# A two-layer decoder trunk: feed-forward operands without the norm's row, quarters formed in PSUM, and two plain gate/up pairs a layer

## Chip, cores and metric

The kernel runs on one core of one Trainium2 chip. The metric is device time in microseconds. The kernel before takes 1182.96 us, the median of 3 runs (1182.89 to 1183.12).

## What is computed

Inputs and output are float32; there are 512 tokens of 1024 channels. Layer 0 mixes tokens by dilated attention, layer 1 by a causal pooling mixer; each is followed by a SwiGLU feed-forward with 2816 hidden channels. Cut to what the change touches:

```python
def rmsnorm(x, g):
    xf = x.astype(jnp.float32)
    y = xf * lax.rsqrt(jnp.mean(xf * xf, axis=-1, keepdims=True) + RMS_EPS)
    return (y * g.astype(jnp.float32)).astype(x.dtype)

def swiglu_ffn(h, w_gate_up, w_down):
    gu = h @ w_gate_up
    gate, up = gu[..., :D_FF], gu[..., D_FF:]
    return (jax.nn.silu(gate) * up) @ w_down

def reference(x, ...):
    for i in range(DEPTH):                       # DEPTH is 2
        ...
            x = x + dilated_attention_mixer(rmsnorm(x, attn_norm[j]), w_qkv[j], w_attn_out[j])
        ...
            x = x + pooling_mixer(rmsnorm(x, pool_norm[j]), w_pool_in[j], w_pool_group[j], pool_scale[j])
        x = x + swiglu_ffn(rmsnorm(x, ffn_norm[i]), w_ffn_gate_up[i], w_ffn_down[i])
    return rmsnorm(x, final_norm)
```

The norm's factor, one over the root of the mean square, is one number per token. With tokens along the free dimension it is a row, and the code calls it `row`.

## The kernel before

**Layout.** Activations stand transposed: `X[k]` holds 128 channels (partitions) by 512 tokens (columns), for k = 0 to 7. Every float32 operand of TensorE (PE) is split into a high and a low part, `split` (L92): ScalarE (ACT) rounds the value to the matmul's type, VectorE (DVE) subtracts. A product then takes three matmuls: high by high, high by low, low by high (L328 to L331, L461 to L463).

**Plain products.** `Product` (L300) multiplies a 128-channel block of weights with all 512 columns of an operand, over k; each matmul has 512 columns. A plain gate/up pair is one such product for 128 gate channels and one for 128 up channels, 8 values of k each.

**Strassen pairs.** `chained` (L521) does a pair of output blocks by Strassen's scheme in Winograd's form: outputs, weights and operands are cut into quarters, and seven multiplications named "11", "1", "2", "21", "3", "22", "4" take the place of eight. Each is `mult` (L457): 4 values of k (K2), three matmuls each, of 256 columns. Three half-banks of PSUM are used, alpha, beta and gamma; ACT copies partial sums out, DVE adds and subtracts them into SBUF tiles (L549, L554, L558). The left operands of the multiplications come from the weights (`Pair`, L157: the corners are loaded, sums of them are formed, each is split). The right ones, in the dictionary `T`, come from quarters of two channel blocks, k and k + 4.

**Preparing the operands.** `prepare` (L1122) makes `T` for one k from normalised activations: `normed` (L576) multiplies `X` by the gain and by `row`, and forms sums and differences; then four splits. As it needs `row`, it comes after the norm. `note` (L396) has by then made the operands of the plain products, gain times `X` without `row`; the plain products multiply by `row` afterwards (L1110, L1116).

**The norm.** `finish` (L436) ends the two or three leading products, and between them computes the row: squares are summed over channels by small matmuls (`rstd`, L403), DVE scales and adds eps (L414), GpSimd takes the power (L417), PE spreads the result (`spread`, L420), ACT copies it (`row_of`, L428).

**A feed-forward layer.** `ffn` (L1100) has 22 gate/up pairs j. The first NPLAIN = 4 are plain, and `prepare(j)` runs beside them; the others are Strassen pairs. The down projection goes in PARTS (L43): channels 0 to 1 plain, 2 to 9 and 10 to 17 as blocks of four `chained` calls each, 18 to 21 plain. Each block is preceded by one more gate/up pair than it needs. `operands`, `operands_right` and `operands_left` (L1149 to L1176) make the right operands of a down block; they wait in a queue `late` and run behind multiplications 4, 5 and 6 of the next `chained` call.

**Order of work.** The program's order is written by hand; engines run in the order that the scheduler fixes when the program is built. Weights flow through rings of buffers (`BUFS`): five of `w`, two of `half`, four of `raw`, two of `rawhalf`. `pump` (L207) issues loads as buffers come free and takes one step of splitting; it is called behind every multiplication. Pairs load over SyncE's queue and accumulate one corner over GpSimd's queue (L173 to L177). Plain weights of the feed-forward are "lean": ACT makes both parts, and a GpSimd DMA accumulates (L149 to L152).

**Where things lie.** Operands get a place from `slot` (L339). With `apart` they begin APART = 28 values (112 bytes) behind the start of a slot, which Strassen operands of the feed-forward use. The weights of a pair begin `shift` values behind the start of their buffer: 0 for the feed-forward (L265, L270), 16 for attention's pairs (L222, except L252), and 16 for the weights of the last five down products (L278).

## Time and profile before

| | |
|---|---|
| median of 3 runs | 1182.96 us |
| the profiled execution's own time | 1183.39 us |
| its span, first to last instruction | 1181.4 us |
| granted clock of TensorE (mean) | 0.999 |
| busy PE, DVE, ACT, GpSimd (POOL) | 1172.5, 993.2, 752.1, 174.9 us |
| moved by DMA | 209.95 MB |

On the page, a group of instructions is a line of code with its engine, what it writes and reads, its shape and its count; then the busy time, the mean duration of one in ns, and the idle time of the engine just before it with what ended it. Matmuls overlap, each record being longer than the distance to the next, so a matmul's price is taken from a stretch of time divided by the number that start in it. In a row of a stretch stand, for each engine, busy us and, in brackets, the number of instructions; then the granted clock of TensorE (1.00 is full), the share of the DMA engines and GB/s.

In layer 0 the long run of Strassen pairs fills about 521 to 769 us of the span, in layer 1 about 902 to 1150.

### The profile page before, as it was taken

The numbers are of one execution on the slowest core, as the hardware profiler recorded it, in microseconds if no ns is written. First come the engines' busy times: TensorE is split into PE (matmuls) and PEld (weight loads), VectorE is DVE, ScalarE is ACT, GpSimd is POOL, SyncE is SP. The second block draws the span as 40 slices with busy tenths as digits, with TensorE's granted clock in tenths as the row PEclk, the third lists the DMA queues.
The fourth block names the chain that finished last, engine by engine and source line by source line (L and its number), as shares of the span: only waits on it lengthen the run. The fifth ranks groups of instructions, "written<-read, shape, count | busy, mean of one in ns | idle before, by whom it ended". The sixth has DMA issues, their size and how long they took to land.

```text
span 1181.4 us, 25585 instructions
## 1 busy us (share of the span) xinstructions
PE 1172.5 (99%) x10182; PEld 1122.5 (95%) x10182; DVE 993.2 (84%) x1747; ACT 752.1 (64%) x1341; POOL 174.9 (15%) x169
## 2 busy tenths in 40 slices
PE   9999999999999999999999999999999999999997
PEld 7899999999999989889999999988889999999997
DVE  8997978989798988799988988657789998898875
ACT  7765665656556666757756766776575776676553
POOL 2111111111111002311111111112130111111100
PEclk9999999999999999999999999999999999999999
DMA  8667656665776557957777777798595777777732
GB/s 291 161 152 198 159 152 146 175 166 143 187 176 148 144 164 204 239 107 200 192 193 194 192 206 189 201 262 207 116 204 116 187 198 196 195 191 194 197 91 72
DMA packets 85017, 209.95 MB, mean 178 GB/s; under 512 B 7953, under 2 KB 13217, under 8 KB 84897
## 3 DMA queue, kind: packets, MB, share of 16 engines
q1 hardware_dynamic: 53104, 145.63, 37.2%
q0 software_dynamic: 31504, 62.41, 32.6%
q8 instruction: 79, 1.29, 0.4%
q14 instruction: 42, 0.34, 0.1%
q10 hardware_dynamic: 288, 0.29, 0.1%
HBM read 206.19 MB, written 2.10 MB: 176 GB/s over the span
## 4 chain that ended last, share of the span: by engine, by line
PE 98%; issue 1%; DVE 0%; POOL 0%; DVEq 0%; POOLq 0%
PE ps L461 21%; PE ps L462 21%; PE ps L463 21%; PE ps L328 7%; PE ps L331 7%; PE ps L329 7%; PE ps L854 2%; PE ps L637 2%; PE ps L638 2%; PE ps L639 2%; PE ps L945 2%; PE ps L732 1%; PE ps L751 1%; PE ps L916 0%; PE ps L836 0%
## 5 line engine op out<-in xcount | busy, mean ns | idle before, releaser
L96 DVE TENSOR_TENSOR w<-raw,w 128x1024 fp32r<-128x1024 f32 x271 | 330.1, 1221 | 46.1 <-ACT w L93 42.1
L93 ACT ACTIVATE w<-raw 128x1024 fp32r<-128x1024 f32 x271 | 285.9, 1062 | 120.6 <-PE ps L463 56.7
L461 PE MATMUL ps<-far,w 128*128 128x256 f32 x896 | 246.5, 275 | 0.0
L462 PE MATMUL ps<-far,w 128*128 128x256 f32 x896 | 246.5, 275 | 0.0
L463 PE MATMUL ps<-far,w 128*128 128x256 f32 x896 | 246.4, 275 | 0.0
L461 PE MATMUL ps<-near,w 128*128 128x256 f32 x749 | 209.5, 280 | 0.0
L462 PE MATMUL ps<-near,w 128*128 128x256 f32 x749 | 207.2, 277 | 0.0
L463 PE MATMUL ps<-near,w 128*128 128x256 f32 x749 | 207.2, 277 | 0.0
L461 PEld LDWEIGHTS ps<-far,w 128*128 128x128 f32 x896 | 168.2, 188 | 0.1
L462 PEld LDWEIGHTS ps<-far,w 128*128 128x128 f32 x896 | 168.2, 188 | 0.1
L463 PEld LDWEIGHTS ps<-far,w 128*128 128x128 f32 x896 | 168.2, 188 | 0.0
L462 PEld LDWEIGHTS ps<-near,w 128*128 128x128 f32 x749 | 141.1, 188 | 0.0
L461 PEld LDWEIGHTS ps<-near,w 128*128 128x128 f32 x749 | 140.7, 188 | 0.1
L463 PEld LDWEIGHTS ps<-near,w 128*128 128x128 f32 x749 | 140.7, 188 | 0.0
L328 PE MATMUL ps<-near,w 128*128 128x512 f32 (+1 forms) x332 | 125.9, 380 | 0.0
L331 PE MATMUL ps<-near,w 128*128 128x512 f32 (+1 forms) x332 | 125.0, 376 | 0.0
L329 PE MATMUL ps<-near,w 128*128 128x512 f32 (+1 forms) x332 | 124.9, 376 | 0.0
L176 POOL DMA_DIRECT2D raw<-w_pair x36 | 43.6, 1210 | 293.4 <-DMA raw<-w_pair 130.9
L329 PEld LDWEIGHTS ps<-near,w 128*128 128x128 f32 x332 | 62.5, 188 | 11.4 <-DVE near L96 0.2
L331 PEld LDWEIGHTS ps<-near,w 128*128 128x128 f32 x332 | 62.3, 188 | 11.5
L328 PEld LDWEIGHTS ps<-near,w 128*128 128x128 f32 x332 | 62.3, 188 | 11.5 <-ACT near L93 0.4
L192 DVE TENSOR_TENSOR raw<-raw 128x512 f32<-128x512 f32 x87 | 59.4, 683 | 5.2 <-issue 5.2
(342 smaller groups left out, 2726.0 us busy)
## 6 DMA issues: line engine op xcount, KB each, us to landing
raw<-w_pair SPq DMA_DIRECT2D x80, 512.0 KB, 5.0
raw<-w_qkp SPq DMA_DIRECT2D x42, 512.0 KB, 4.5
raw<-w_pair POOLq DMA_DIRECT2D x36, 512.0 KB, 7.6
raw<-w_dblock SPq DMA_DIRECT2D x32, 512.0 KB, 4.4
raw<-w_qkp POOLq DMA_DIRECT2D x21, 512.0 KB, 7.7
rawhalf<-w_pair SPq DMA_DIRECT2D x36, 256.0 KB, 5.2
raw<-w_v SPq DMA_DIRECT2D x16, 512.0 KB, 4.1
raw<-w_dblock POOLq DMA_DIRECT2D x16, 512.0 KB, 7.7
```

The lines of the kernel that those rows point to most:

```text
L93: made = nc.scalar.activation(hi, v, AF.Copy)
L96: nc.vector.tensor_tensor(lo, v, hi.bitcast(F32), op=OP.subtract)
L176: nc.gpsimd.dma_start(self.b.rearrange("p (a c) -> p a c", a=2), self.src[:, None, 3 * n:].to_broadcast([P, 2, n]), accum_op=OP.add)
L192: nc.vector.tensor_add(a[:, :n], a[:, :n], b[:, :n])
L328: nc.tensor.matmul(self.p[:, cols], w[0][:, s], mh[:, cols], start=self.done == 0, stop=False)
L329: nc.tensor.matmul(self.p[:, cols], w[0][:, s], ml[:, cols], start=False, stop=False)
L331: nc.tensor.matmul(self.p[:, cols], w[1][:, s], mh[:, cols], start=False, stop=self.done == self.n)
L461: nc.tensor.matmul(dst, w.t[0][:, c], th, start=k == 0 and not on, stop=False, skip_group_check=on)
L462: nc.tensor.matmul(dst, w.t[0][:, c], tl, start=False, stop=False, skip_group_check=on)
L463: nc.tensor.matmul(dst, w.t[1][:, c], th, start=False, stop=k == n - 1, skip_group_check=on)
L637: nc.tensor.matmul(o, mh, wh, start=k == 0, stop=False)
L638: nc.tensor.matmul(o, mh, wl, start=False, stop=False)
```

## The change

**No row in the operands.** `prepare` now takes an operator number and works from `X` and the gains alone. "11", "21" and "22" are quarters of the operands that `note` made; only the four sums are formed and split. It can therefore run ahead of the norm: three of four `prepare` calls stand before `finish` and one behind it. In layer 1 they stand between the steps of the pooling mixer, and the channel blocks are paired in another order (`ORDER`), with the weights reordered to match when the inputs are laid out.

**The row comes in at the gate.** The gate is multiplied by `row` before Silu; up is not. The hidden values are then too large by one over `row`, so the residual stream is brought to the same scale: `grow` multiplies every `X[m]` by the reciprocal of `row`, half of them behind each of the pairs j = 2 and 3. The next norm removes the scale, with an eps of its own for each token (`floor`, passed as `least`). Before the pooling mixer `X` is multiplied by the old row.

**Quarters form in PSUM.** In `chained`, ACT copies alpha into beta, and DVE writes b - d into gamma; multiplications "21" and "22" accumulate on them. What the caller does with the finished halves is passed in as `ready`: multiplying by the row and Silu for a gate, adding to `X` for a down block. Beta is one bank for the whole layer, `kept`, which held a leading product first.

**Two plain pairs.** NPLAIN is 2; pairs 2 and 3 are Strassen pairs and still come before the first plain down part (`FIRST` = 4).

**Places and order.** The feed-forward's weights lie 16 values behind the start (the default of `pairs`), its operands at the start. The negated operand "22" is gone: the last weights of a gate/up pair are split with the sign turned. The first merge of attention stands behind multiplication 3 of head 1, not 1. The variance operation always goes first. Special order of the very last pair (`first`, `right`) is gone.

```diff
-NPLAIN = 4
+NPLAIN = 2
+FIRST = 4
+ORDER = {3: (0, 2, 4, 6, 1, 3, 5, 7)}
...
+    nneg = cpool.tile([P, NORMS, KC], F32, name="nneg")
+    floor = cpool.tile([P, NT], F32, name="floor")
...
         def last(self):
-            self.take("l", "half", self.c)
+            if self.turned:
+                self.w["l"] = w = Held("half", self.shift)
+                w.n = self.n
+                split_neg(*(t[:, :self.n] for t in w.t), self.c)
+            else:
+                self.take("l", "half", self.c)
...
-                    pairs(w_pair[layer, j], shift=0, back=True)
+                    pairs(w_pair[layer, j], back=True, turned=True)
...
-        with tc.high_priority() if r is not None else nullcontext():
-            nc.vector.tensor_scalar(v, pc[:, :nt], 1.0 / D, EPS, op0=OP.mult, op1=OP.add)
+        with tc.high_priority():
+            if least is None:
+                nc.vector.tensor_scalar(v, pc[:, :nt], 1.0 / D, EPS, op0=OP.mult, op1=OP.add)
+            else:
+                nc.vector.scalar_tensor_tensor(v, pc[:, :nt], 1.0 / D, least, op0=OP.mult, op1=OP.add)
+        if keep:
+            nc.vector.tensor_scalar(floor, v, EPS, None, op0=OP.mult)
...
-        alpha, beta, gamma = (ps()[:, :H2] for i in range(3))
-        ab, cd = scratch("first"), scratch("sums")
-        a, b, c, d = ab[:, left], ab[:, right], cd[:, left], cd[:, right]
+        alpha, gamma = (ps()[:, :H2] for i in range(2))
+        beta = kept[:, :H2]
+        bs, cd = scratch("first"), scratch("sums")
+        b, c, d = bs[:, left], cd[:, left], cd[:, right]
...
-        nc.scalar.copy(a, alpha)
+        nc.scalar.copy(beta, alpha)
...
         nc.scalar.copy(b, alpha)
+        nc.vector.tensor_sub(gamma, b, d)
...
-        mult(beta, wb, 1, T, "21", n)
+        mult(beta, wb, 1, T, "21", n, on=True)
         wb.done()
-        nc.vector.tensor_add(one[:, left], beta, a)
+        ready(left, beta)
...
-        nc.vector.tensor_sub(one[:, right], b, gamma)
+        ready(right, gamma)
...
-                    return {1: [later(merge, h - 1)]} if odd else {2: [later(output, h - 2), later(merge, h - 1)]}
+                    return {3 if h == 1 else 1: [later(merge, h - 1)]} if odd else {2: [later(output, h - 2), later(merge, h - 1)]}
...
+        def prepare(op, k):
+            a, b = (ORDER.get(op, range(KC))[i] for i in (k, k + K2))
+            ga, gb, gn = nrm[:, op, a:a + 1], nrm[:, op, b:b + 1], nneg[:, op, b:b + 1]
+            T["11", k] = halves_of(*operand[op, a])[0]
+            T["21", k], T["22", k] = halves_of(*operand[op, b])
+            h, t = ftile("ha"), Temp()
+            nc.scalar.activation(h, X[a], AF.Copy, scale=ga)
+            one, two, three, four = (t.t[:, i * H2:(i + 1) * H2] for i in range(4))
+            nc.vector.tensor_sub(one, h[:, H2:], h[:, :H2])
+            nc.vector.scalar_tensor_tensor(two, X[b][:, H2:], gn, one, op0=OP.mult, op1=OP.add)
+            nc.vector.scalar_tensor_tensor(three, X[b][:, H2:], gb, h[:, H2:], op0=OP.mult, op1=OP.subtract)
+            nc.vector.scalar_tensor_tensor(four, X[b][:, :H2], gb, two, op0=OP.mult, op1=OP.add)
+            for i, names in enumerate((("1", "2"), ("3", "4"))):
+                held["t", k, i], v = slot("tt", top=True)
+                split(v[:, 0], v[:, 1], t.t[:, i * S:(i + 1) * S])
...
                 nc.vector.tensor_mul(gt, pg, row)
-                prepare(j)
+                nc.scalar.activation(gt, gt, AF.Silu)
                 pu = gu()
...
-                nc.vector.tensor_mul(up, pu, row)
-                nc.scalar.activation(gt, gt, AF.Silu)
-                nc.vector.tensor_mul(up, up, gt)
+                nc.vector.tensor_mul(up, pu, gt)
+
+            def grow(ms):
+                if "std" not in U:
+                    U["std"] = ftile("std")
+                    nc.vector.reciprocal(U["std"], row)
+                for m in ms:
+                    nc.vector.tensor_mul(X[m], X[m], U["std"])
...
-                held["d", name, i], b = slot("d" + name, apart=True)
+                held["d", name, i], b = slot("d" + name)
...
+                def gate(half, p):
+                    nc.vector.tensor_mul(gt[:, half], p, row[:, half])
+                    nc.scalar.activation(gt[:, half], gt[:, half], AF.Silu)
+
+                left = chained(T, u, ftile, K2, kept, gate, inner=True, after=hooks)
...
+                    if NPLAIN <= j < FIRST:
+                        grow(range((j - NPLAIN) * K2, (j - NPLAIN + 1) * K2))
...
-                        one, two = ftile("one"), ftile("two")
-                        chained(D, one, two, ftile, (end - first) // 2, after=waiting())
...
+                        two = ftile("two")
+                        def add(half, p):
+                            nc.vector.tensor_add(X[m][:, half], X[m][:, half], p)
+                        chained(D, two, ftile, (end - first) // 2, kept, add, after=waiting())
+                        down(m + 1, two, last)
...
         lead = begin(2, 1, range(KC - 1))
-        row = finish(lead, 1, [KC - 1])
+        kept = ps()
+        for k in range(K2 - 1):
+            prepare(1, k)
+        row = finish(lead, 1, [KC - 1], kept, keep=True)
+        prepare(1, K2 - 1)
...
-        row = finish(lead, 2, range(KC - 2, KC))
+        for m in range(KC):
+            nc.vector.tensor_mul(X[m], X[m], row)
+        row = finish(lead, 2, range(KC - 2, KC), least=floor)
...
-        lead = begin(2, 3, range(4, KC))
+        lead = begin(2, 3, (2, 3, 6, 7))
+        prepare(3, 3)
+        prepare(3, 2)
         mix(0)
...
+        prepare(3, 1)
+        row = finish(lead, 3, (0, 4), keep=True)
+        prepare(3, 0)
```

118 lines of the change are left out of this document (39 added, 79 removed).

## The prediction

> **What bounds the kernel now.** I read the page first, for who is busy and whether TensorE's clock is whole; then the list of PE's waits, for what a removed wait could give; then the stretches ("windows") of the two kinds of feed-forward work, for the price of one matmul; last the timelines of DVE where the change puts new work.
>
> ```profile
> span 1181.4 us, 25585 instructions
> PE 1172.5 (99%) x10182; PEld 1122.5 (95%) x10182; DVE 993.2 (84%) x1747; ACT 752.1 (64%) x1341; POOL 174.9 (15%) x169
> PEclk9999999999999999999999999999999999999999
> PE 98%; issue 1%; DVE 0%; POOL 0%; DVEq 0%; POOLq 0%
> ```
>
> PE is busy for 99% of the span at an undiminished clock, and 98% of the chain that ended last is PE's own work. A busy PE is not yet proof, as its records overlap; so the waits:
>
> ```profile
> PE ps L916 <- DVE idle L913: 1.2, 1, 1.2
> PE ps L782 <- PE ps L463: 1.0, 1, 1.0
> PE ps L782 <- DVE far L770: 0.3, 1, 0.3
> ```
>
> Three waits, 2.5 us in all. In the two feed-forward layers PE waits for nobody. So a change gains what it takes out of PE's stream, and loses whatever pace or waits it puts in. The price of a matmul, in stretches long enough to divide:
>
> ```profile
> core 0: us, PE busy (x) PEld busy (x) DVE busy (x) ACT busy (x) POOL busy (x), PEclk, DMA share, GB/s
> 481.00:519.00 38.00, 38.00 (x169) 31.46 (x168) 37.90 (x66) 24.33 (x38) 8.01 (x7) 1.00 0.86 174
> 522.00:594.00 72.00, 72.00 (x638) 72.00 (x637) 64.97 (x121) 50.25 (x91) 8.48 (x7) 1.00 0.72 185
> 232.90:250.00 17.10, 17.10 (x153) 17.10 (x152) 16.99 (x28) 9.19 (x18) 3.11 (x3) 1.00 0.76 182
> 1157.60:1165.80 8.20, 8.20 (x72) 8.20 (x71) 5.01 (x11) 3.13 (x7) 0.00 (x0) 1.00 0.01 3
> ```
>
> The count takes in those that were under way when the stretch began: about 2.4 of the short ones (275 ns long, started every 113), 1.7 of the 512-column ones. The first row is plain products: 38.00 / 167.3 = 227.1 ns for 512 columns. The second is Strassen pairs: 72.00 / 635.6 = 113.3 ns for 256. The third and fourth rows come back among the rivals.
>
> **The matmuls removed.** A plain gate/up pair is two products of 8 blocks by 3 matmuls: 48 x 227.1 = 10.90 us. A Strassen pair is 7 x 4 x 3 = 84 short ones: 84 x 113.3 = 9.52 us. NPLAIN from 4 to 2 converts two pairs in each of two layers: 4 x 1.38 = **5.5 us gained**, all of it on PE's path. The other pairs, and the down products, keep their matmul counts.
>
> Beside the row, the Trainium skill ("TensorE: Matmul & The Clock Gate", Back-to-back issue gap) gives N / 2.4 + 2.5 ns a matmul, an isolated gap of 215.8 and 109.2 ns; by it the four pairs would give 4 x 1.19 = 4.7 us. The rows stand 5% and 4% above it, and I keep the rows.
>
> **The first merge, two multiplications later** (slot 3 in place of 1 for head 1):
>
> ```profile
> 56.59 0.28 PE L463 MATMUL ps<-near,w 128*128 128x256 f32 x1
> 56.95 0.69 DVE L516 TENSOR_TENSOR vt<-ps,sums 128x512 f32<-128x512 f32 x1
> 57.55 0.21 DVE L770 TENSOR_TENSOR far<-st,place 128x64 f32<-128x64 f32 x1
> 57.87 0.41 PE L782 MATMUL ps<-far,const 128*128 128x64 f32 x2 [1.00 <-PE ps L463]
> ```
>
> PE started L782 1.28 us after the matmul before it, where 0.11 is normal, because DVE came to L770 only at 57.55. Two multiplications are 24 x 113.3 = 2.7 us; they cover the 1.17. **1.2 us gained.** Bounds: 0 to 1.2; I take all, as cover is twice the wait.
>
> **The chained products.** Beta and gamma now finish in PSUM: ACT copies alpha into beta, DVE writes b - d into gamma, PE accumulates on top. That is one more 256-wide DVE operation a gate/up pair (six for five), the same number of ACT copies, Silu in two halves. DVE's prices, from starts that follow each other without a gap:
>
> ```profile
> 539.41 1.22 DVE L96 TENSOR_TENSOR w<-raw,w 128x1024 fp32r<-128x1024 f32 x1
> 540.55 0.69 DVE L192 TENSOR_TENSOR raw<-raw 128x512 f32<-128x512 f32 x1
> 541.15 0.42 DVE L1207 TENSOR_TENSOR u<-u,gt 128x256 f32<-128x256 f32 x1
> 541.49 0.42 DVE L1208 SCALAR_TENSOR_TENSOR u<-ps,gt 128x256 f32<-128x256 f32 x1
> 541.82 0.68 DVE L193 TENSOR_TENSOR raw<-raw 128x512 f32<-128x512 f32 x1
> ```
>
> So 1.14 us for 1024 columns, 0.60 for 512, 0.34 for 256. In the Strassen stretch above DVE is busy 64.97 of 72 us with 72 / 9.52 = 7.6 pairs; 7.6 x 0.34 = 2.6 more makes 94%. It still fits, on average. The new waits are on PE: "21" needs the ACT copy from 1.36 us earlier, and "22" needs gamma = b - d, where b exists only after "2".
>
> ```profile
> L545 ACT COPY first<-ps 128x256 f32<-128x256 f32 x52 | 19.1, 368 | 32.4 <-PE ps L463 32.4
> ```
>
> Between the end of "2" and "22" lie two multiplications, 2.7 us. Against that: a copy of 0.37, at most one split under way on DVE, 1.14, and the subtraction, 0.42: 1.9 us. Cover of 0.8 us; if DVE is a second split behind, PE waits 0.3 us, and behind PE's wait stand all later multiplications of the pair. I price this at 0 in the steady run (bounds 0 to 0.3 x 56 pairs = 17 us; the nearest row is the Strassen stretch, where DVE still idles a tenth).
>
> **Operands without the row.** Prepare no longer multiplies by the row and takes "11", "21", "22" from the operands that exist; it issues four 256-wide operations and two 512-wide splits, 4 x 0.34 + 2 x 0.60 = 2.6 us of DVE, where L581 to L592 with four splits took about twice that. It moves ahead of the row, so is there room?
>
> ```profile
> 475.57 0.16 DVE L414 TENSOR_SCALAR var<-ps 128x4 f32<-128x4 f32 x1 [6.78 <-PE ps L410]
> ...
> 850.08 0.75 DVE L1337 SCALAR_TENSOR_TENSOR x<-ps,nrm,x 128x512 f32<-128x512 f32 x1 [2.69 <-PE ps L331]
> 851.44 0.75 DVE L1337 SCALAR_TENSOR_TENSOR x<-ps,nrm,x 128x512 f32<-128x512 f32 x1 [0.61 <-PE ps L331]
> ...
> 857.36 0.16 DVE L414 TENSOR_SCALAR var<-ps 128x4 f32<-128x4 f32 x1 [2.64 <-PE ps L410]
> ```
>
> Layer 0: 6.8 us idle against three prepares of 2.6 = 7.7, and DVE had further holes before; cost 0. Layer 1: 2.69 + 0.61 + 2.64 = 5.9 idle against 7.7; two of the prepares stand ahead of mix(0), whose scaled operands PE needs next. 1.8 us do not fit; bounds 0 and 1.8 us, I take half: **0.9 us lost**. The variance operation is put first now, so it does not queue behind prepares.
>
> **Grow.** Eight 512-wide multiplications a layer (8 x 0.60 = 4.8 us) and a reciprocal, whose width the trace lacks:
>
> ```profile
> L1315 DVE TENSOR_TENSOR_SCAN s<-u 128x512 f32<-128x512 f32 x4 | 4.9, 1221 | 0.1
> ```
>
> I put it between a plain 512-wide operation, 0.6, and this slowest one, 1.2. They fall behind the two new Strassen pairs, so a pair there needs of DVE: preparation of a weight pair 3 x 1.14 + 3 x 0.60 = 5.2, six chained operations 2.0, half of grow 2.7 to 3.0, together 9.9 to 10.2 us in 9.52 of PE. Over by 0.4 to 0.7 us a pair; the first group of grow stands just ahead of the next pair's gamma. PE may lose 0 to 1.4 us a layer; I take 0.3, as weights are prepared ahead and the following down products leave DVE room: **0.6 us lost**. The plain stretch shows why I lean low: there DVE is full, 37.90 of 38, and PE loses nothing.
>
> X times the old row before the pooling mixer: 8 x 0.60 = 4.8 us.
>
> ```profile
> 801.36 0.16 DVE L414 TENSOR_SCALAR var<-ps 128x4 f32<-128x4 f32 x1 [7.12 <-PE ps L410]
> ```
>
> It goes into 7.1 idle us, and the row is overwritten only after that: 0. The eps that is carried along, the negated gains, the turned "l": 0, hidden on DVE and ACT beside PE.
>
> **Sum.** -5.5 - 1.2 + 0.9 + 0.6 = -5.2 us. The profiled execution took 1183.39 (span 1181.4 and 2.0 around it), 0.43 above the median of 1182.96. Against its own time 1178.2, against the median **1177.8 us**, 0.44% faster.
>
> **Rivals.** *The slower pace (ends slower).* The change also moves operands in SBUF: weights go from the start of their buffer to 16 values (64 bytes) behind it, operands from 28 values to none. Attention's pairs and the last products already lie so (weights at 16, operands at 0), and they show two paces at the same granted clock 1.00: the third row gives 17.10 / 150.6 = 113.5 ns, the fourth 8.20 / 69.6 = 117.8. A stretch that enters the slow pace keeps it until something interrupts PE, and the fourth row was entered straight from 512-column products, as a feed-forward run would be. For: that placement. Against: the third row, equally placed; also, the two new small tiles push every later buffer by some 52 values, so no row has the exact placement. Price: 4.5 ns a matmul. One layer's long run is 26 pairs, 2184 matmuls, 9.8 us: 1177.8 + 9.8 = 1187.6. All 56 pairs: 21 us, 1199. It decides from 5.2 / 0.0045 = 1160 matmuls, a quarter of the 4704. Chance 0.17, of which 0.13 end slower. The Trainium skill ("SBUF — State Buffer", Who interferes with whom) gives PE two independent read ports, for the moving operand and for weights, that contend with nobody; by it this rival would not exist. The two paces at one clock say that something does.
>
> *DVE becomes the bound around the two new pairs.* For: 9.9 to 10.2 us of need in 9.52, prepare and the next weights close by. Against: the full DVE of the plain stretch, without a wait of PE. If the 1.4 and 1.8 us above show in full, and gamma waits 0.3 us in a dozen pairs: 2.8 + 1.8 + 3.6 - 1.5 (counted already) = 6.7 more. At the full price that is 1184.5, at half 1181.2; either lies within 0.2% of now. Chance 0.13.
>
> *It gains more.* The shift by 52 values may lift attention's 27 calls of 84 matmuls out of the slow pace; if a third of them stands in it now, an estimate from those two rows, that is 0.33 x 2268 x 4.5 ns = 3.4 us: 1174.4. Chance 0.08.
>
> *The pairs are converted but no time comes.* If a short matmul cost over 10.90 / 84 = 0.130 us, a converted pair would be no shorter than a plain one; with the merge's gain and the two losses that is 1182.96 - 1.2 + 1.5 = 1183.3. The Trainium skill (same section of the TensorE page) has sustained figures of 131 ns at 512 columns and about 81 at 128, by which 48 long ones cost 6.3 us and 84 short ones at least 6.8. The rows say 227.1 and 113.3, in proportion to the columns; chance 0.01.
>
> **How the numbers follow.** Forecast as summed 0.61, more gain 0.08, DVE 0.13, slow pace 0.17, no time 0.01. A measurement of this kernel can tell about 0.2% (2.4 us) from no change. Faster: 0.61 + 0.08 + 0.02 of the slow pace that touches only the short runs = 0.71; same 0.13; slower 0.16. The range reaches from the gain in attention, 1174.0, to one long run at the slow pace, 1187.6.
>
> **What would show it.** In the profile after: 192 fewer 512-column matmuls and 336 more short ones; Strassen stretches that still divide to 113.3 ns; no wait at L782's successor near 57 us; DVE without its idle stretches before the variance; reciprocal and grow near 500 and 880 us. The prediction is wrong if the short matmuls come every 117 ns or more, or if PE's list of waits names DVE at gamma's multiplication.

## The result, and the profile after

The changed kernel takes **1219.52 us**, the median of 3 runs (1219.14 to 1220.12), against 1182.96 (1182.89 to 1183.12) before. The ratio is 1.0307 (95% interval 1.0293 to 1.0322): 3.1% slower, where 0.4% faster was forecast, and far outside the range. The profiled execution took 1219.14 us, with a span of 1217.1: 35.7 us more than before's.

From the page of the kernel after: the span, the busy time of each engine, and the chain that ended last.

```profile
span 1217.1 us, 26047 instructions
...
PE 1200.3 (99%) x10326; PEld 1155.0 (95%) x10326; DVE 1028.8 (85%) x1820; ACT 750.6 (62%) x1389; POOL 172.5 (14%) x161
...
PE 89%; issue 4%; DMA 3%; DVE 2%; POOL 1%; ACT 1%; POOLq 0%; DVEq 0%; ACTq 0%
```

PE has 144 matmuls more (10326 for 10182: 192 long ones fewer, 336 short ones more), as the change says. By their prices they take 5.5 us less; PE is nevertheless busy for 28 us longer. And its share of the chain has fallen from 98% to 89%, with DMA, DVE and GpSimd now in it. So there are two things to find, a dearer matmul and new waits. The waits of PE after (who waits, for whom; us in total, times, longest). A name such as `ps` is the PSUM tile that the waiting matmul writes:

```profile
PE ps L339 <- DMA w<-w_down: 5.0, 4, 1.8
PE ps L437 <- POOL rcol L430: 2.9, 2, 2.4
PE ps L418 <- DVE sq L391: 1.3, 1, 1.3
PE ps L931 <- DVE idle L928: 1.2, 1, 1.2
PE ps L797 <- DVE far L785: 0.2, 1, 0.2
```

The last line is the first merge, with 0.2 us where 1.3 stood: that part came. The first three lines are new, 9.2 us. The stretches after, in the columns of the prediction's rows: two inside the long Strassen runs of layers 0 and 1, and the stretch of attention that stood at 232.90 before.

```profile
545.00:617.00 72.00, 72.00 (x614) 72.00 (x613) 67.40 (x127) 48.32 (x96) 8.45 (x7) 1.00 0.77 187
930.00:1002.00 72.00, 72.00 (x613) 72.00 (x613) 68.61 (x131) 48.13 (x98) 8.47 (x7) 1.00 0.73 179
235.84:252.94 17.10, 17.10 (x148) 17.10 (x147) 15.63 (x26) 9.17 (x18) 2.54 (x2) 1.00 0.81 184
```

Before, 638 matmuls were counted in 72 us and 153 in 17.1; now 614 and 148, at the same granted clock of 1.00 and with PE busy throughout. In the long runs that is 72.00 / 611.6 = 117.7 ns a matmul for 113.3, in both layers; in attention about 117.4 for 113.5. In each of these stretches PE is busy for the whole time, before and after, so its busy share shows nothing of it; the count in a stretch does.

Where the 35.7 us lie, from the starts of all matmuls in the two traces:

| part | us |
|---|---|
| four pairs converted, by counts and prices | -5.5 |
| wait at the first merge, 1.3 to 0.2 | -1.1 |
| 4704 feed-forward matmuls, 113.37 to 117.63 ns on average | +20.0 |
| 2899 short matmuls of attention, 114.6 to 117.3 ns | +7.7 |
| stall at the spread of layer 0's row, and slow matmuls behind it | +4.9 |
| stalls at the first down parts, likewise (5.1 and 2.3) | +7.4 |
| last square of layer 1's norm | +1.4 |
| sum (0.9 not placed) | +34.8 |

### The profile page after: what moved, and what is told of

Same layout as the page of the kernel before. It is cut to its first block, busy times and chain, and to the rows that moved or that the text cites. A ratio compares the mean times of both kernels' runs of the same rounds, so it can differ in the third digit from the quotient of the medians.

```text
span 1217.1 us, 26047 instructions
## 1 busy us (share of the span) xinstructions
PE 1200.3 (99%) x10326; PEld 1155.0 (95%) x10326; DVE 1028.8 (85%) x1820; ACT 750.6 (62%) x1389; POOL 172.5 (14%) x161
## 4 chain that ended last, share of the span: by engine, by line
PE 89%; issue 4%; DMA 3%; DVE 2%; POOL 1%; ACT 1%; POOLq 0%; DVEq 0%; ACTq 0%
PE ps L474 21%; PE ps L476 21%; PE ps L475 21%; PE ps L339 4%; PE ps L336 4%; PE ps L337 4%; PE ps L869 2%; PE ps L652 2%; PE ps L654 2%; PE ps L653 2%; PE ps L960 2%; DMA raw<-w_pair 1%; DMA w<-w_down 1%; PE ps L747 1%; PE ps L766 1%
## 5 line engine op out<-in xcount | busy, mean ns | idle before, releaser
L97 ACT ACTIVATE w<-raw 128x1024 fp32r<-128x1024 f32 x283 | 297.6, 1059 | 161.1 <-PE ps L476 75.4
L100 DVE TENSOR_TENSOR w<-raw,w 128x1024 fp32r<-128x1024 f32 x283 | 344.5, 1219 | 49.7 <-ACT w L97 47.2
L474 PE MATMUL ps<-near,w 128*128 128x256 f32 x1069 | 302.4, 283 | 0.0
L475 PE MATMUL ps<-near,w 128*128 128x256 f32 x1069 | 300.0, 281 | 0.0
L476 PE MATMUL ps<-near,w 128*128 128x256 f32 x1069 | 299.7, 280 | 0.0
L475 PEld LDWEIGHTS ps<-near,w 128*128 128x128 f32 x1069 | 203.4, 190 | 0.2
L474 PEld LDWEIGHTS ps<-near,w 128*128 128x128 f32 x1069 | 201.4, 188 | 0.3
L476 PEld LDWEIGHTS ps<-near,w 128*128 128x128 f32 x1069 | 201.3, 188 | 0.0
L474 PE MATMUL ps<-far,w 128*128 128x256 f32 x672 | 189.1, 281 | 0.0
L475 PE MATMUL ps<-far,w 128*128 128x256 f32 x672 | 188.7, 281 | 0.0
L476 PE MATMUL ps<-far,w 128*128 128x256 f32 x672 | 188.7, 281 | 0.0
L475 PEld LDWEIGHTS ps<-far,w 128*128 128x128 f32 x672 | 128.9, 192 | 0.0
L474 PEld LDWEIGHTS ps<-far,w 128*128 128x128 f32 x672 | 126.1, 188 | 0.2
L476 PEld LDWEIGHTS ps<-far,w 128*128 128x128 f32 x672 | 126.1, 188 | 0.0
L339 PE MATMUL ps<-near,w 128*128 128x512 f32 (+1 forms) x268 | 101.4, 379 | 5.0 <-DMA w<-w_down 5.0
L336 PE MATMUL ps<-near,w 128*128 128x512 f32 (+1 forms) x268 | 102.3, 382 | 0.0
L337 PE MATMUL ps<-near,w 128*128 128x512 f32 (+1 forms) x268 | 100.9, 377 | 0.0
L180 POOL DMA_DIRECT2D raw<-w_pair x40 | 49.6, 1239 | 325.8 <-ACT w L97 90.4
L196 DVE TENSOR_TENSOR raw<-raw 128x512 f32<-128x512 f32 x91 | 62.1, 683 | 6.6 <-DMA raw<-w_pair 2.7
L339 PEld LDWEIGHTS ps<-near,w 128*128 128x128 f32 x268 | 50.9, 190 | 16.1 <-DMA w<-w_down 6.7
L197 DVE TENSOR_TENSOR raw<-raw 128x512 f32<-128x512 f32 x91 | 62.1, 683 | 0.1
L337 PEld LDWEIGHTS ps<-near,w 128*128 128x128 f32 x268 | 51.2, 191 | 9.0 <-DVE near L401 0.2
```

Source lines behind the costliest of these rows:

```text
L97: made = nc.scalar.activation(hi, v, AF.Copy)
L100: nc.vector.tensor_tensor(lo, v, hi.bitcast(F32), op=OP.subtract)
L180: nc.gpsimd.dma_start(self.b.rearrange("p (a c) -> p a c", a=2), self.src[:, None, 3 * n:].to_broadcast([P, 2, n]), accum_op=OP.add)
L196: nc.vector.tensor_add(a[:, :n], a[:, :n], b[:, :n])
L197: nc.vector.tensor_add(a[:, n:], a[:, n:], a[:, :n])
L336: nc.tensor.matmul(self.p[:, cols], w[0][:, s], mh[:, cols], start=self.done == 0, stop=False)
```

## Experiments

Two theories. **Places**: where operands and weights begin in SBUF sets the pace of the short matmuls; the stalls are separate. **The changed work**: accumulating in PSUM, the gate's reads of it or DVE's longer stream slow PE; the places are innocent. Single runs here stand beside a run of before at 1183.1 to 1183.5 us on the same chip.

### Moving buffers and nothing else

An unused tile behind the constants moves every later buffer: in before by 224 bytes, as the two new small tiles do in after; in after by 32 more, so that the buffers begin where they began in before, modulo 256 bytes. (Where operands lie inside their buffers in the feed-forward stays as in after.)

```diff
 # e2_before_moved (before)
+    pad = cpool.tile([P, 56], F32, name="pad")
+    nc.vector.memset(pad, 0.0)
 # e1_pad (after)
+    pad = cpool.tile([P, 8], F32, name="pad")
+    nc.vector.memset(pad, 0.0)
```

> The kernel before with one unused tile of 56 values (224 bytes) behind its small tiles: only addresses differ. Theory 1: attention slows by 7 to 8 us as in the changed kernel, and the feed-forward's long runs, with operands at 80 and weights at 96 bytes modulo 128, may leave 113.3 ns; 1188 to 1215 us. Theory 2: 1182 to 1184 us.

> The changed kernel with one more small tile of 8 values (32 bytes) behind its two new ones, so that all later buffers lie 256 bytes further than in the kernel before, and no longer 224. Nothing else differs. Theory 1 (the pace of a 256-column matmul follows from where its two operands begin, modulo 128 bytes): attention lies as in the kernel before again and returns to its pace, 7 to 8 us faster in front of the feed-forward; the feed-forward's pairs have operands at 0 and weights at 64 bytes, the placing of attention, and run either at 113.3 or at 117.8 ns, so in all 1190 to 1212 us. Theory 2 (the pace comes from accumulating on what ACT and DVE wrote into PSUM, or from DVE's load): no change in attention beyond 1 us, 1218 to 1220 us.

Before, moved: 1195.38 us, 12 us slower with not an instruction of its computation changed. Its rows for the same stretch of attention, and for the long run of layer 0:

```profile
240.26:257.36 17.10, 17.10 (x148) 17.10 (x147) 15.62 (x26) 9.18 (x18) 2.54 (x2) 1.00 0.76 180
545.00:617.00 72.00, 72.00 (x638) 72.00 (x637) 64.54 (x116) 50.66 (x88) 8.78 (x8) 1.00 0.74 193
```

Attention counts 148, as in after; the feed-forward still counts 638. After, moved back: 1213.17 us, attention at 114.5 ns again, the feed-forward still at 117.6. So attention's part of the loss is the 224 bytes. The spare tile's own operation has a side effect: in both runs PE waited near 30 us for the first norm's result (a gap of 3.0 and 2.6 us between two matmuls), which neither before nor after has. Without that, the move is worth about 9 us in either direction (in before 11.9 less 3.0 slower, in after 6.4 and 2.6 faster).

### Before with the feed-forward placed as in after

```diff
-                    pairs(w_pair[layer, j], shift=0, back=True)
+                    pairs(w_pair[layer, j], back=True)
 # the same for w_dblock
-            o = APART * apart
+            o = 0 * apart
 # the same for the other line with APART * apart
```

> Before, with the feed-forward pairs' operands at the start of their slots and their weights 64 bytes into their buffers, which is how the changed kernel places them relative to each other; nothing else differs from before. Theory (places set the pace): 52 pairs of 84 matmuls at 117.6 ns in place of 113.3, 18 to 20 us more: 1201 to 1204 us, and no PE waits that before hasn't. Rival (the new forms of the changed kernel slow its matmuls): 1183.4 us, the same as before within 1 us.

1201.38 us. The rows of the long run of layer 0 and of attention:

```profile
545.00:617.00 72.00, 72.00 (x614) 72.00 (x613) 61.18 (x106) 47.14 (x82) 8.47 (x7) 1.00 0.70 181
232.90:250.00 17.10, 17.10 (x154) 17.10 (x152) 15.33 (x24) 9.46 (x18) 2.54 (x2) 1.00 0.77 183
```

614 in the feed-forward, and no new wait; attention, not moved, counts 154 (before: 153). The operands and weights lie as after's do inside their buffers (in bytes modulo 256 they begin at 128 and 192, as in after moved back; after itself has 96 and 160). Before's own instructions run there at after's pace: 52 x 84 x 4.4 ns = 19.2 us, of which 18.3 show. **So the slow pace comes without any of the changed work.** That it also goes with the changed work in place is shown further down, by e10_place.

### Other places

```diff
 # e3_map (after): the weights of each feed-forward pair shifted by another amount
+        shifts = iter([2 * p if layer == 0 else 2 * ((11 * p + 3) % 32) for p in range(28)])
-                    pairs(w_pair[layer, j], back=True, turned=True)
+                    pairs(w_pair[layer, j], shift=next(shifts), back=True, turned=True)
 # e5_place (after, e1's tile): every slot 112 bytes in, feed-forward weights at 0
-        o = APART * apart
+        o = APART
 # e5_zero: e5_place, and attention's weights at 0 as well
-    def pairs(*srcs, shift=LINE // 4, back=False, turned=False):
+    def pairs(*srcs, shift=0, back=False, turned=False):
 # e8_place: feed-forward operands alone 112 bytes in; gaps of 32 values in the near room for it
```

> The changed kernel with another start for the weights of each Strassen pair of the feed-forward: 2 values (8 bytes) further from pair to pair in layer 0, the same starts in a mixed order in layer 1. Operands stay. Theory 1: the pace of a pair follows its start: some pairs near 113.3, others near 117.8 ns, with the start of 16 values (64 bytes from the operands) among the slow ones and the starts near 4 values (16 bytes behind the operands, the distance in the kernel before) among the fast ones; 1200 to 1215 us. Theory 2: all pairs at 117.8 ns, 1219 us.

> After, with every matmul operand held in a slot moved 112 bytes into it, 8 spare values behind floor so that all buffers stand at the same places modulo 256 bytes as in before, and the feed-forward pairs' weights at the start of their buffers: the feed-forward products then read operands and weights from the places (modulo 128 bytes) from which before's read them, 112 and 0. Nothing computed changes. Theory (places set the pace): the 256-column matmuls of the feed-forward pairs come every 113.2 to 113.5 ns in place of 117.6, some 4,600 of them, so 19 to 21 us less than the run with the spare tile alone (1213.2): 1192 to 1195 us, if attention keeps its 114.5 ns, and up to 7 us more if its new places (112 and 64) are slow ones. Rival (the accumulation in PSUM, the gate's reads of it or VectorE's longer stream slow the matmuls): 117.6 ns stays, 1212 to 1214 us.

> The kernel of the run before this one (operands 112 bytes into their slots), with the weights of attention's pairs at the start of their buffers too, so that most of attention's 256-column matmuls also have the places 112 and 0. Theory (places set the pace): attention at 113.3 to 114 ns on those, so 2 to 6 us below the other run, about 1188 to 1192 us. Rival (attention's pace is set by its own course, not by places): the same time as the other run within 1 us.

> After, with every place as in before: 8 spare values behind floor, two gaps of 32 values in the near room, attention's operands at the start of their slots, and the feed-forward's operands 112 bytes into theirs with their weights at 0. In the run that had moved attention's operands too, attention's 256-column matmuls came every 118.4 ns (at 112 and 64) in place of 114.7 and its 512-column products lost 16.2 us in waits. Theory (places set the pace): attention 114.5 to 115 ns, feed-forward 113.4 ns, so 19 to 21 us below the 1213.2 us of the run with the spare tile alone as far as the pace goes; and of that the waits for the first down parts' weights and for the variance take back 2 to 5 us, since a faster TensorE comes to them sooner: 1194 to 1200 us. Rival (a pace that the changed kernel's own work sets): attention above 116 ns or feed-forward above 116 ns, over 1204 us.

e3_map 1221.42, e5_place 1206.51, e5_zero 1205.68, e8_place 1223.75 us. e3_map missed its forecast of 1200 to 1215: a pair's mean ran from 113.3 to 121.0 ns with its shift, and only 3 of the 56 pairs were at 113.4 or below. Two of these had after's own shift of 16 values, which had been expected among the slow ones. In e5_place the feed-forward came at 113.4 ns, but attention went to 118.1; e5_zero, with attention's weights at 0, had 116.8 on average where the operand stood in the near room and 118.3 or more where it lay in X's old tiles. The forecast of 1192 to 1195 for e5_place failed mainly for that, about 10 us against after moved back. Two smaller things stood beside it: a long matmul took 229.9 ns on average for 227.7, some 2 us, and the wait at attention's first norm grew. The waits for the first down parts were as in after, 5.0 us, although the feed-forward was faster:

```profile
PE ps L341 <- DMA w<-w_down: 5.0, 4, 2.2
PE ps L439 <- POOL rk L432: 3.0, 1, 3.0
```

e8_place was to put everything back (1194 to 1200 us was expected). Its short matmuls had before's places modulo 128 bytes; but the longer near room had moved the weights by 128, modulo 256. Its matmuls came slow in both layers and in attention, 512-column ones at 231 ns and more for 227:

```profile
600.00:672.00 72.00, 72.00 (x620) 72.00 (x619) 61.26 (x103) 44.81 (x83) 9.67 (x8) 1.00 0.74 189
```

Collected over the runs, feed-forward pairs by the places of operand and weights in bytes modulo 256 (mean distance of starts, those over 130 ns left out):

| operand, weights | run | ns |
|---|---|---|
| 240, 128 | before, e5_place, and the two e10 runs below | 113.4 |
| 208, 96 | before, moved | 113.4 |
| 128, 192 | before placed as after; after, moved back | 117.8; 117.6 |
| 96, 160 | after | 117.6 |
| 112, 0 and 240, 0 | e8_place | 116.4 and 117.3 |

No rule comes out of it. 112 bytes of distance is fast at 240/128 and slow at 112/0; in attention 128/192 runs at 114.6 to 114.8, in the feed-forward at 117.6. And it is not the places alone, as e9_order below shows.

### Order

The stalls first, as after's trace has them. At 485 us PE waits some 2.4 us for the spread of layer 0's row. The squares' matmuls, and then DVE:

```profile
L418 PE MATMUL ps<-ones,sq x32: 170/170/191, 481.9 to 482.1; 128*32 128x1 f32 x32
```

```profile
480.44 0.69 DVE L196 TENSOR_TENSOR raw<-raw 128x512 f32<-128x512 f32 x1 [1.86 <-issue]
...
482.25 0.42 DVE L1127 TENSOR_TENSOR temp<-ha 128x256 f32<-128x256 f32 x1
...
484.16 1.29 DVE L100 TENSOR_TENSOR far<-temp,far 128x512 fp32r<-128x512 f32 x2 [0.18 <-ACT far L97]
...
486.23 0.48 DVE L1128 SCALAR_TENSOR_TENSOR temp<-x,nneg,temp 128x256 f32<-128x256 f32 x1
486.62 0.15 DVE L423 TENSOR_SCALAR var<-ps 128x4 f32<-128x4 f32 x1
```

The sums were ready at 482.3, the variance ran at 486.62, 4.3 us later (before: 0.1). DVE's order was fixed when the program was built: pieces of prepare (L1127 to L1130) stand ahead of it, and they stand behind L196, which sat for 1.86 us. The row names nothing that it waited for (`issue`); the load of its weights, issued by GpSimd at 471.27, landed at 480.36, just ahead of its start. Then, at the first down part, PE and GpSimd:

```profile
519.02 0.40 PE L337 MATMUL ps<-near,w 128*128 128x512 f32 x1
521.23 0.50 PE L339 MATMUL ps<-near,w 128*128 128x512 f32 x1 [1.81 <-DMA w<-w_down]
...
523.13 0.63 PE L336 MATMUL ps<-near,w 128*128 128x512 f32 x1
523.56 0.63 PE L337 MATMUL ps<-near,w 128*128 128x512 f32 x1
```

```profile
509.30 1.31 POOL L156 DMA_DIRECT2D w<-w_down  x1 [2.06 <-PE ps L476]
521.52 1.29 POOL L156 DMA_DIRECT2D w<-w_down  x1 [10.91 <-ACT w L97]
```

Each DMA brings half of the part's lean weights. PE's wait at 519 ends when the first has landed, at 521.18, 11.9 us after its issue; the second, issued at 521.52, lands at 529.9 and is awaited from 528.2. The two don't overlap: in all 16 such pairs of before, after, e1_pad, e3_map, e5_place, e5_zero, e8_place and e10_place the second was issued 0.34 or 0.35 us behind the landing of the first. So such a part needs two landings in a row, 14 to 21 us from the first issue in before and after. Before, the two were issued at 492.94 and 502.58, the second landed at 508.71, and the down part began near 509. What moved them towards their use is, by the order of the steps, that the weights of pairs 2 and 3 are now Strassen weights, with four steps each, ahead of them in the list; that was read from the code and not tried by itself. Behind this wait matmuls start every 427 ns for some 3 us, and behind the one at the spread for 1.7. The granted clock of the former:

```profile
522.60:526.20 3.60, 3.60 (x11) 2.82 (x10) 2.02 (x4) 0.00 (x0) 1.42 (x2) 0.53 0.66 121
```

So a wait of 2 us cost 1.6 us more at half the clock. Two starts 2.2 and 2.8 us apart were followed by this; where two starts were 1.1 to 1.7 us apart (at 528, 881, 915 and 921 us) the matmuls behind came every 226 to 236 ns, but for the first at about 335, and the granted clock stayed at 1.00 behind the waits at 528, 915 and 921. The Trainium skill ("TensorE: Matmul & The Clock Gate", Wait — 56ns, not 53.3ns?) has 426.7 ns a 512-column matmul at the halved clock, which agrees. The Trainium skill ("TensorE: Matmul & The Clock Gate", What's actually happening) lets the clock fall after an idle window of about 3.4 us; in this trace PE stood for 2.0 when it fell.

```diff
 # e4_stalls: the first down part's weights split on DVE; layer 0's prepares traced behind finish
-                                lean=layer == 0 or first == 0,
+                                lean=layer == 0 and first > 0,
 # e9_order: that, layer 1's prepares behind finish too, and on DVE behind the variance
+        with tc.issue_after(made[0]):      # made[0] is the variance operation
+            for k in range(K2):
+                prepare(1, k)
 # e6_all: e5_place with e4_stalls' edits in both layers; e9_all: e8_place with e9_order
```

> The changed kernel with layer 0's prepare calls all behind finish, and with the weights of the first down part split on DVE in both layers and not accumulated by a GpSimd DMA. Theory 3 (DVE's variance operation stood behind prepare and a late load; the second accumulating DMA of the first down part was issued only when the first had landed): the waits at 485 us and at 519, 528, 915 and 921 us go, together about 10 us with the slow clock behind them, 1208 to 1212 us; the pace stays at 117.8 ns. If the waits were the new pairs' weights arriving late, they stay, 1217 to 1221 us.

> The first kernel of this call (operands at 112 bytes, feed-forward weights at 0), and beside it: layer 0's four prepares behind finish, layer 1's four prepares behind finish too (behind mix(0) and the last squares), and the first down part's weights split on VectorE instead of with an accumulating DMA, in both layers. Theory (places for the pace, and three stalls of TensorE that stand beside it): 7.2 us for the first two, as the run with them alone showed, and 1.3 us for the wait at the last square of layer 1, so 8 to 9 us below the first kernel of this call, 1183 to 1187 us. Rival (the stalls would move, since the slower pace gave VectorE time that it now lacks): less than 4 us below it, with TensorE's waits on VectorE behind finish in place of those removed.

> After, at its own places, with three edits of order: the first down part's weights split on VectorE in both layers; layer 0's and layer 1's prepares all behind finish; and VectorE's share of each prepare queued behind the operation for the variance. Theory (the variance stood in VectorE's fixed order behind the prepares and the pair sum; the accumulating DMAs were late): the waits of 2.8 us at spread, of 2.2, 1.7, 1.1 and 1.5 us at the first down parts and of 1.3 us at the last square are gone, with the slow matmuls behind them some 13 us: 1205 to 1208 us. The run that had split the weights on VectorE, but had the prepares behind finish without the order on VectorE, took 1211.96 and still waited 3.4 us at spread. Rival (VectorE is simply full there): the waits at spread go, and come back within the first four gate/up pairs as waits of TensorE on VectorE: 1210 us or more.

> The first kernel's places and the second's order together. Theory (places and three stalls are all that the change lost by): before's time less the 5.5 us of the converted pairs and the 1.2 us of the moved merge, plus up to 3 us for what VectorE has now to do behind finish: 1176 to 1181 us. Rival (something else of the change costs as well): over 1185 us, and the place where it is lost shows in the times of TensorE's stages.

e4_stalls 1211.96, 7.6 us below after. The waits for weights are gone, which the table has at 7.4. The one at the spread stayed, 3.0 us: being traced later did not take the prepares out of the variance's way. e6_all 1204.62, 2 us below e5_place where 8 were expected, with 4.0 us at the spread: my reading of e4_stalls, that it had removed that wait, was wrong. e9_order **1203.35**, below the 1205 to 1208 expected, at after's own places: no wait at the spread, the variance 0.1 us behind the squares; in exchange PE waits at the first pairs, 4.5 us in all, as the rival had it in part:

```profile
PE ps L476 <- ACT sums L570: 1.9, 1, 1.9
PE ps L476 <- ACT ps L553: 1.4, 1, 1.4
...
PE ps L476 <- ACT far L97: 1.2, 1, 1.2
```

And it gained more than its waits, because the pace of layer 0 changed. Its rows of layer 0 and layer 1, and of two shorter stretches at the start of layer 1:

```profile
575.00:647.00 72.00, 72.00 (x638) 72.00 (x637) 63.41 (x107) 45.76 (x85) 9.71 (x8) 1.00 0.76 191
1010.00:1082.00 72.00, 72.00 (x614) 72.00 (x613) 64.24 (x115) 47.88 (x93) 9.45 (x8) 1.00 0.74 188
912.30:930.20 17.90, 17.90 (x155) 17.90 (x154) 17.28 (x34) 10.77 (x22) 1.20 (x1) 1.00 0.56 128
931.40:949.90 18.50, 18.50 (x166) 18.50 (x164) 17.94 (x36) 12.55 (x28) 2.43 (x2) 1.00 0.83 206
```

The same places in the same kernel, 113.3 ns in one layer and 117.7 in the other. So a place like this one has two paces. The starts of the matmuls show that a run keeps its pace until PE's stream is broken. In layer 1 here the mean distance is 117.8 ns up to 930.4 us, 113.4 from 931.2 to 950.0, and 117.8 from there on; between the first two stand distances of 409 and 221 ns, between the others one of 215. After's own trace has it too: 2123 matmuls at 117.8 ns from 535.1 us on, two distances of 138 and 229 ns at 785.1, and then 113.6. So has before's, in its last products: 117.8 ns in the prediction's fourth row, about 113.5 behind the squares that follow, 117.8 again behind the spread.

After entered four runs of over 100 matmuls straight from 512-column products, and all four were slow; a run of e9_order at 527.5 us, entered the same way, was fast. What decides the pace at a break stays open. e9_all, with e8_place's places, took 1214.67 where 1176 to 1181 was expected; its pace was slow in both layers.

### The short matmuls' places as in before, and the stalls taken out

e10_place has the places of all short matmuls as in before modulo 256 bytes. (375 of its long ones read their operand at 240, where before had 128: the plain products share the operands of the Strassen pairs now.) e10_all adds a measured order: one prepare of each layer ahead of finish, three behind the variance; first down weights split on DVE. e12_best takes out what the experiments had brought in, and spreads grow over the first down part.

```diff
 # e10_place (after): spare tile of 200 values behind floor; near room 128 values longer,
 # gaps of 64 values behind its slots 7 and 9; feed-forward slots with apart=True, weights shift=0
 # e10_all: and
+        prepare(1, 0)
         row = finish(lead, 1, [KC - 1], kept, keep=True)
+        with tc.issue_after(made[0]):
+            for k in range(1, K2):
+                prepare(1, k)
 # e12_best: and, in place of the spare tile,
+    floor = cpool.tile([P, NT + 204], F32, name="floor")[:, :NT]
 # plain hidden operands without apart; each X[m] grown just ahead of its first addition
```

> The run that was to put every place back (attention's operands at the start of their slots, the feed-forward's 112 bytes into theirs) had moved the weights' buffers by 128 bytes against the operands' room, modulo 256, and all its matmuls came slow: 117.4 ns in attention, 116.5 in the feed-forward, 231 ns for 512 columns. Here every place is as in before modulo 512 bytes: a spare tile of 200 values behind floor, gaps of 64 values in the near room, which is 128 values longer. Nothing else differs from after. Theory (places modulo 256 bytes or more set the pace): attention 114.7 ns, feed-forward 113.4, 512 columns 227; with the stalls of after, which grew to 16 us in the run with the feed-forward at 113.3 ns: 1192 to 1200 us. Rival (the pace isn't set by places of buffers as far as they are told apart here): over 1204 us.

> The kernel of the run before this one, and beside it the three edits of order in another measure: the first down part's weights split on VectorE; one prepare of each layer ahead of finish and three behind it, queued on VectorE behind the operation for the variance. With all four behind it, TensorE waited 2.3 us for the first pair's operands in layer 0 and 3.0 in layer 1, and one prepare is some 3.2 us of VectorE. Theory (places and the stalls are all that the change lost by): before's 1183.2 us less 5.5 and 1.2, plus 1 to 4 us for what is left of the stalls: 1178 to 1181 us. Rival (the change costs something else): 1185 us or more, with TensorE's stages showing where.

> The last kernel (all places as in before, stalls taken out) less what the experiments themselves had put in or left: the spare tile is a longer floor, without an operation of its own, which in the other runs had delayed the first norm of attention (TensorE waited 1.3 us for its result, and over 3 us in others); the hidden values of the plain down products lie at the start of their slots again, as in before (227 in place of 231 ns for 512 columns, some 200 of them, 0.9 us); and the growing of X is spread over the first down part, each block just ahead of its first addition, where VectorE has room, in place of four at once behind each of the two pairs (waits of 1.4 and 0.8 us). Theory (places and stalls are all that the change lost by): 1187.1 less 4 us, 1182 to 1184 us, within 0.2% of before; what the pairs gained is then still spent, by the waits that are left. Rival (the change has a cost of its own that no stall shows): no gain on the last kernel, 1186 us or more.

e10_place: **1200.11** us, 0.1 above what was expected. The same stretches once more:

```profile
545.00:617.00 72.00, 72.00 (x638) 72.00 (x637) 68.45 (x129) 47.88 (x97) 8.45 (x7) 1.00 0.77 192
237.44:254.54 17.10, 17.10 (x153) 17.10 (x152) 17.07 (x28) 9.20 (x18) 3.07 (x3) 1.00 0.78 185
```

638 and 153, exactly before's counts, with all of the changed work in place. With the run of before at after's offsets, this shows **the places, and not the changed work, as the cause of the pace**. By the table of the 35.7 us the two paces are worth 27.7; of that, 19.0 show between the two profiled executions. Of the 8.7 missing, the wait at the first norm is new (3.2 us), the first down parts' weights are awaited for 6.4 us in place of 5.0, and the long matmuls' mean, 228.9 ns for 227.6, makes about 1; the rest was not placed.

e10_all: 1187.12 us (7 runs, 1184.57 to 1188.23), ratio 1.003 to before (1.0019 to 1.0042). 32 of the 37 us are back. But my 1178 to 1181 was too low, and by the expectation's own words the result lies on the rival's side (1185 or more: the change costs something else). What its trace shows is two gaps of 1.4 and 0.8 us at the first pairs, one of 1.7 at attention's first norm and about 400 long matmuls at 231 ns. e12_best takes these on. 

e12_best: **1181.80** us (11 runs, 1181.15 to 1183.21) against 1183.49 (15 runs, 1182.49 to 1185.71), ratio 0.9986 (0.9977 to 0.9995). That is 0.14% below before and a little below what was expected, and speaks for the theory; the interval excludes no change only just, and the prediction took 0.2% for the least that can be told apart, so it is best read as before's time regained. Of the 3.7 us between its profiled execution and e10_all's, 3.1 lie ahead of the end of attention, where the spare tile's operation had been in the way. Layer 1 is shorter by 0.9 and layer 0 by nothing; spreading grow and moving the plain hidden operands both act there and were not tried apart. Its waits:

```profile
PE ps L477 <- ACT sums L571: 1.3, 2, 0.8
PE ps L934 <- DVE idle L931: 1.2, 1, 1.2
PE ps L800 <- DVE far L788: 0.3, 1, 0.3
```

The span of its profiled execution is 2.4 us below before's. The counts and the merge give 6.6; 3.4 go in gaps between short matmuls, 2.8 of it in layer 0 between 480 and 560 us; 0.8 go in 192 long ones that read from the other place at 231 ns, 0.5 in a mean pace of 113.48 for 113.37. That leaves 1.9, and attention gives 0.4. So the counts and the merge give what was forecast, and more than half of it is spent on waits and places.

## Why the prediction was wrong, point by point

- **The matmuls removed**: right in kind and size. With the places restored the price of 113.3 holds, and that of 227 for the long matmuls that stand where before's stood. **The first merge**: right, 1.1 of 1.2 us came.
- **The step that failed: "The slower pace", held at 0.17, with a range that ends at one long run, 9.8 us.** The sum held the pace of the short matmuls at 113.3 ns. What came in its place is 117.6 in both layers and 117.3 in attention, 27.7 us in all; with the places of before, e10_place has the old counts again. The mechanism was named, with its two paces, its price of 4.5 ns and its sign, and it was rightly said that a stretch keeps the slow pace until something interrupts PE; for 56 pairs 21 us were given, and 20.0 came. But it was made a rival where the row nearest to the case was slow, and the range stopped at one long run. The reason against it was one fast row of attention with equal distances. That row says a fast pace is possible there, not that a run entered from 512-column products would get it; the row that was entered so was slow. What decides the pace at a break was not known then and isn't now, so which layers it would hit could not be told.
- **The two small tiles were taken for a chance of gain.** "It gains more" had the shift (52 values by its count, 56 or 224 bytes as built) lift attention; it cost attention 7.7 us. Nothing in the profile gave that a sign, and the working should have carried it with both.
- The Trainium skill ("SBUF — State Buffer", Who interferes with whom) says that PE never waits on anyone, and by that this rival had no time at all. Before with its buffers moved, about 9 us slower, and before with the feed-forward placed as in after, 18 us slower, say that a place can cost PE 4% of a stretch.
- **Prepare ahead of the norm in layer 0, priced at 0.** The working added up DVE's idle time, 6.8 us, and took it that "the variance operation is put first now". The fixed order put prepare's pieces in front of it: 4.9 us. e9_order, with the pieces behind it, has no such wait. In layer 1, 0.9 was forecast and 1.4 came.
- **The first down parts were not in the sum.** It counted the instructions of the two new pairs and not when the down part's weights would be issued: 7.4 us, gone in e4_stalls. That the new pairs' steps pushed them back is read from the code.
- **Grow.** The reciprocal was bounded by 0.6 and 1.2 us; it takes 3.34 (below). In e10_all PE's gaps at grow are 1.4 and 0.8 us, where 0.6 was forecast for both layers. The one in layer 1 has the sign that the prediction named, gamma late on DVE: its subtraction (L565) stood behind four of grow's multiplications.

```profile
886.40 2.49 DVE L1163 TENSOR_TENSOR x<-x,std 128x512 f32<-128x512 f32 x4
888.81 0.43 DVE L565 TENSOR_TENSOR ps<-first,sums 128x256 f32<-128x256 f32 x1
889.29 0.38 PE L479 MATMUL ps<-near,w 128*128 128x256 f32 x1 [0.45 <-DVE ps L565]
```

The one in layer 0 ended with a copy of ACT's, which stood behind a split that had waited 2.6 us for a weight load; it is not DVE's alone. So "DVE becomes the bound" was half right: not at gamma's multiplication in the steady run, which cost nothing (0 was taken), but around finish and where grow stands.

## What to carry to other kernels

Before an edit that moves buffers or adds a small tile is priced, count matmuls in a stretch of known length in several places of the trace: two paces at one clock mean that placing is part of the price, with both signs. A control run that only moves buffers, or only restores them, tells it from the work. What is put ahead of a norm's variance must be weighed by its position in the engine's order, not by idle time; and for each step inserted into a list of weights, ask what stands behind it in that list and when that is due.

## What the hardware showed beside this

The reciprocal of 128x512 float32 on DVE, after:

```profile
L1156 DVE RECIPROCAL std<-row x2: 3341/3341/3341, 505.3 to 901.0; 128x512 f32<-128x512 f32 x2
L1158 DVE TENSOR_TENSOR x<-x,std x16: 677/680/684, 510.7 to 918.3; 128x512 f32<-128x512 f32 x16
```

It takes 4.9 times a multiplication of the same shape. The second accumulating DMA of a pair of lean loads was issued 12.2 us after the first although ACT had made its parts by 511.24 us. It followed the landing of the first by 0.34 us, as in the 16 pairs above; the trace records no wait on that landing, and why it holds stays open. The 512-column matmuls too have places at 231 and at 227 ns: in e12_best 170 with operand and weights at 240 and 128 took 230.9 ns on average, 535 at 128 and 128 took 227.4.
